# Value heads 1 to 3 of the gated linear branch as one job of seven half-size products

## The chip, the cores and the metric

The kernel runs on one core of a Trainium2 chip. The metric is the device time of one execution in microseconds (us). A core has a matrix engine (TensorE, PE in the profile; PEld are its weight loads), a vector engine (DVE), a scalar engine (ACT), GpSimd (POOL) and SyncE (SP), which here issues the DMA transfers. Each engine works through its own list of instructions in order and waits on semaphores for the others. Matrix products accumulate in PSUM banks; everything else is held in SBUF.

## The reference

One layer of a decoder with two parallel token mixers, for 1024 tokens and a width of 1024, in float32:

```
h = rmsnorm(x, norm_g)
proj = h @ w_in                        # one wide projection, split into
g_q, g_k, g_v, g_gate, g_rank, s_q, s_k, s_v, s_gate, m_logits
log_a = log_sigmoid(g_rank @ w_dec_up + b_dec) / 16
o_gla = gla_chunked(g_q, g_k, g_v, log_a)          # 4 heads, values of 256
o_gla = rmsnorm(o_gla, gla_norm_g) * silu(g_gate);  y_a = o_gla @ w_pa
o_sb = stick_breaking(s_q, s_k, s_v) * silu(s_gate); y_b = o_sb @ w_pb
merged = g_a * y_a + g_b * y_b                      # sigmoid gates
x = rmsnorm(x + merged @ w_o, final_g)
```

The case is about g_v, the values of the first branch: h (1024 x 1024) times 1024 columns of w_in, four heads of 256 columns. The decay code g_rank has 16 columns and rides along with head 0.

## The kernel before

**Precision.** Every float32 factor is split into a high half (ACT, L163: a copy to the matmul's type, names ending in h) and a low half (DVE, L164: the value minus its high half, names ending in l). A product is three matmuls: high x high, high x low, low x high.

**First stage (0 to 44.6 us).** For each of eight blocks of 128 tokens (tb): ACT sums the squares, DVE scales the sum, POOL takes the power -1/2 (L229, a tile r of 128 x 1), DVE multiplies by r and the gain (L397, xs), PE transposes (L417), and ACT and DVE split the result into the quarters of h. There are four quarters, by half of the tokens and by parity of the 128-wide feature blocks: A11, A12, A21, A22, named ha11, ha12, ha21, ha22 in the trace, each with four blocks j. One block behind, PE computes head 0 with the decay code for the previous block (272 columns). ACT's and DVE's order is that of the code; the other engines' order is set by the scheduler at build time.

**The value heads 1 to 3 (44.6 to 113.8 us).** 24 units, one for each head and token block, are plain projections (L221): 24 matmuls of 256 columns each, tokens on the output's partitions, eight feature blocks deep. DVE splits each result straight out of PSUM and SP stores it. Meanwhile POOL makes sums of the quarters of h that later jobs need: A11, A12, A21, A22 as whole values (L502, high plus low) and S1, S2, S3, S4 from them (L505), 32 operations of 512 elements a row; ACT and DVE split the S.

**The pairs (from 113.8 us).** All other projections are jobs of two heads that use seven products of half size instead of eight (Winograd's form of Strassen's scheme): weights as the stationary side, sums T1 to T4 of weight quarters made on POOL (L241 to L244, tt), seven units per job, 512 columns a matmul. Between the units of the first jobs stand the decay steps: `wup`, the decay's up-projection, is loaded (L655), put into a stack (`wst`, L668 and L670), the decay codes are transposed (L677) and split into `rst`, and L684 multiplies both (logits). Job 0's loads and its first three splits stand at the head, ahead of the decay steps.

Of the kernel before, what the change touches and what calls it, by code (L numbers as in the profile page):

```python
# [101 lines left out]
def hybrid_layer(ctx: ExitStack, tc: tile.TileContext, x, norm_g, w_in, w_up, b_dec,  # L102
# [355 lines left out]
    vw = v_ctx.enter_context(tc.tile_pool(name="vw", bufs=2, reuse_waits="tile"))  # L458
    vws, vraw = {}, {}

    def v_load(c0, key):
        vraw[key] = raw_tile()
        nc.sync.dma_start(vraw[key], w_in[:, c0:c0 + DV].rearrange("(k p) c -> p k c", p=P))

    def v_split(key, i):

        hi, lo = ((vw.tile([P, 4, DV], F32R, tag="v" + s, name="v" + s) if i else
                   w_tile(s).rearrange("p k c -> p (k c)").rearrange("p (k c) -> p k c", c=DV)) for s in "hl")
        split(vraw[key][:, 4 * i:4 * i + 4], hi, lo)
        vws.setdefault(key, []).append((hi, lo))  # L470
# [10 lines left out]
    vjobs = [(i, C_GV + i * DV) for i in range(1, GLA_H)]  # L481
    v_load(vjobs[0][1], vjobs[0][0])
    v_load(vjobs[1][1], vjobs[1][0])
    vline = []
    for i, (key, _) in enumerate(vjobs):
        for tb in range(NT):
            vline.append((lambda key=key, tb=tb: v_unit(key, tb), True))
            if tb in (3, 4) and i + 1 < len(vjobs):
                vline.append((lambda key=vjobs[i + 1][0], a=tb - 3: v_split(key, a), False))
# [1005 lines left out]
```

## Time and profile before

| | |
|---|---|
| time, median of 3 runs | 1190.39 us (1189.76 to 1190.4) |
| profiled execution, span | 1187.3 us |
| PE busy | 1174.5 us (99%) |
| DVE busy | 834.8 us (70%) |
| POOL busy | 294.4 us (25%) |
| value heads 1 to 3 | 576 matmuls, 69.33 us |

The profiled execution is shown by its span; no other time of it is recorded, and the runs are about 3 us longer than the span. A row of a timeline has the start, the time of the instruction or group, engine, line, operation, tiles (written, then read), shape, and count; in square brackets the idle time of the engine before it and what ended that. L numbers are lines of the kernel before. In the changed kernel the same helpers have other numbers (split is L160 and L161, the power L226).

### The profile page before, as it was taken

The page shows a single profiled execution, that of the slowest core. Times are in us where ns is not written, and L with a number is a line of the kernel's source. Part 1 is how long each engine was busy: PE and PEld are TensorE (multiplying, and loading weights), DVE is VectorE, ACT ScalarE, POOL GpSimd, SP SyncE. Part 2 cuts the span into 40 slices and gives each one's busy share as a digit, 9 for nine tenths or more (in the row PEclk, how much of TensorE's full clock was granted, in tenths as well). Part 3 has the DMA queues.
Part 4 walks back from the last instruction along what each step waited for, and adds up shares of the span by engine and source line. Part 5 has one row for each costly group of instructions (what it writes and reads, how often), then busy time and mean ns, then how long its engine had stood idle before and what let it go on. Part 6 is the DMA issues. An engine that isn't in the chain of part 4 may idle for free.

```text
span 1187.3 us, 17020 instructions
## 1 busy us (share of the span) xinstructions
PE 1174.5 (99%) x6051; PEld 989.3 (83%) x6051; DVE 834.8 (70%) x1388; ACT 535.3 (45%) x1000; POOL 294.4 (25%) x249
## 2 busy tenths in 40 slices
PE   8999999999999999999999999999999999999997
PEld 8999878888888888888888887888888888888886
DVE  6475876787677777767656567547787876488986
ACT  5343763333444444444434444334444544275543
POOL 1496513143333233224223223000000000700001
PEclk9999999999999999999999999999999999999999
DMA  7434349998356566655454447899766556848652
GB/s 286 196 133 153 129 164 317 331 316 275 120 187 222 183 213 215 188 187 169 145 168 149 133 138 229 254 322 320 258 218 224 186 168 192 288 160 285 220 195 106
DMA packets 189377, 247.65 MB, mean 209 GB/s; under 512 B 12358, under 2 KB 121948, under 8 KB 187756
## 3 DMA queue, kind: packets, MB, share of 16 engines
q1 hardware_dynamic: 188716, 245.52, 61.6%
q8 instruction: 47, 0.77, 0.3%
q10 hardware_dynamic: 576, 1.05, 0.2%
q14 instruction: 38, 0.31, 0.1%
HBM read 154.25 MB, written 92.27 MB: 208 GB/s over the span
## 4 chain that ended last, share of the span: by engine, by line
PE 89%; DVE 4%; ACT 2%; DMA 2%; issue 1%; SPq 0%; POOL 0%; ACTq 0%; DVEq 0%
PE pp L268 15%; PE pp L269 15%; PE pp L270 15%; PE pp L221 8%; PE pp L204 3%; PE pp L203 3%; PE pp L202 3%; PE tr L990 1%; PE av L1013 1%; PE av L1012 1%; PE av L1011 1%; PE z L972 1%; PE z L974 1%; PE z L973 1%; PE xb L1379 1%
## 5 line engine op out<-in xcount | busy, mean ns | idle before, releaser
L164 DVE TENSOR_TENSOR wl<-tt,wh 128x1024 fp32r<-128x1024 f32 x62 | 77.5, 1250 | 53.2 <-ACT wh L163 52.9
L307 DVE TENSOR_TENSOR f<-pp,f 128x512 f32<-128x512 f32 x93 | 64.0, 688 | 72.1 <-PE pp L270 68.2
L242 POOL TENSOR_TENSOR tt<-raw 128x512 f32<-128x512 f32 x31 | 44.6, 1438 | 225.2 <-DVE wl L164 204.8
L163 ACT ACTIVATE wh<-tt 128x1024 fp32r<-128x1024 f32 x62 | 65.6, 1058 | 74.7 <-PE pp L269 68.8
L274 ACT ACTIVATE f<-pp 128x512 f32<-128x512 f32 x93 | 55.1, 593 | 88.2 <-PE pp L270 84.9
L978 DVE TENSOR_TENSOR_SCAN be<-be,m 128x128 f32<-128x128 f32 (+3 forms) x64 | 86.1, 1347 | 4.5 <-ACT be L975 4.3
L163 ACT ACTIVATE wh<-raw 128x1024 fp32r<-128x1024 f32 x44 | 46.5, 1059 | 84.0 <-PE pp L269 48.1
L164 DVE TENSOR_TENSOR wl<-raw,wh 128x1024 fp32r<-128x1024 f32 x44 | 64.3, 1463 | 18.7 <-ACT wh L163 18.1
L229 POOL TENSOR_TENSOR r<-r,nhalf 128x1 f32<-128x1 f32 x40 | 24.4, 609 | 198.3 <-DVE r L228 177.2
L1162 POOL TENSOR_TENSOR N<-A,A 128x512 f32<-128x512 f32 x4 | 6.6, 1658 | 244.0 <-PE pp L204 244.0
L975 ACT ACTIVATE be<-z 128x384 f32<-128x384 f32 (+4 forms) x96 | 47.1, 495 | 19.7 <-PE z L974 17.3
L268 PE MATMUL pp<-ha11h,wh 128*128 128x512 f32 x124 | 49.2, 397 | 0.0
L268 PE MATMUL pp<-S2h,wh 128*128 128x512 f32 x124 | 49.1, 396 | 0.0
L268 PE MATMUL pp<-S1h,wh 128*128 128x512 f32 x124 | 49.1, 396 | 0.0
L268 PE MATMUL pp<-ha12h,wh 128*128 128x512 f32 x124 | 49.0, 395 | 0.0
L268 PE MATMUL pp<-ha22h,wh 128*128 128x512 f32 x124 | 48.9, 394 | 0.2 <-DVE f L307 0.2
L268 PE MATMUL pp<-S3h,wh 128*128 128x512 f32 x124 | 48.8, 394 | 0.0
L268 PE MATMUL pp<-S4h,dh 128*128 128x512 f32 x124 | 48.6, 392 | 0.0
L270 PE MATMUL pp<-S1h,wl 128*128 128x512 f32 x124 | 48.4, 390 | 0.0
L270 PE MATMUL pp<-ha11h,wl 128*128 128x512 f32 x124 | 48.4, 390 | 0.0
L269 PE MATMUL pp<-S2l,wh 128*128 128x512 f32 x124 | 48.3, 390 | 0.0
L270 PE MATMUL pp<-ha12h,wl 128*128 128x512 f32 x124 | 48.3, 390 | 0.0
(519 smaller groups left out, 3844.4 us busy)
## 6 DMA issues: line engine op xcount, KB each, us to landing
raw<-in_w_in_dram SPq DMA_DIRECT2D x34, 1024.0 KB, 6.0
d_gv<-o SPq DMA_DIRECT2D x16, 512.0 KB, 2.6
d_t<-t SPq DMA_DIRECT2D x16, 512.0 KB, 6.4
v<-d_gv SPq DMA_DIRECT2D x32, 256.0 KB, 3.0
d_ogl<-o SPq DMA_DIRECT2D x64, 128.0 KB, 2.6
d_q<-o SPq DMA_DIRECT2D x16, 512.0 KB, 3.8
d_k<-o SPq DMA_DIRECT2D x16, 512.0 KB, 3.5
d_v<-o SPq DMA_DIRECT2D x32, 256.0 KB, 2.5
```

The lines of the kernel that those rows point to most:

```text
L163: nc.scalar.activation(hi, src, AF.Copy)
L164: eng.tensor_sub(lo, src, hi.bitcast(F32))
L202: nc.tensor.matmul(pt, whi[:, kb], h_, start=kb == 0, stop=False)
L221: nc.tensor.matmul(pt[:, 0:n], *ops[kb][i], start=k == 0, stop=k == 3 * KB - 1)
L242: nc.gpsimd.tensor_sub(t1, b[:, 0, 1], b[:, 0, 0])
L268: nc.tensor.matmul(pt, bh[:, j], ah[:, j], start=first and j == 0, stop=False, skip_group_check=True)
L269: nc.tensor.matmul(pt, bh[:, j], al[:, j], start=False, stop=False, skip_group_check=True)
L270: nc.tensor.matmul(pt, bl[:, j], ah[:, j], start=False, stop=j == 3, skip_group_check=True)
L274: nc.scalar.activation(t[nm], t[bank], AF.Copy)
L307: nc.vector.tensor_add(add, bank, add)
L975: nc.scalar.activation(om[:, off + pc * w:off + (pc + 1) * w], zt[:, 0:w], AF.Sigmoid, scale=-inv_sqrt)
L978: nc.vector.tensor_tensor_scan(rest, rest, m1[:, off:T][:, ::-1], 1.0, op0=ALU.mult, op1=ALU.max)
```

## The change

Heads 1 to 3 become one job of 768 columns, computed with the same seven-product scheme, but with tokens on the output's partitions: the features are the stationary side and the weights move. Weight quarters are B11, B12, B21, B22 (parity of the feature block by half of the columns, 384 each). A product u has two halves (jp, two feature blocks each) of four token blocks t: 56 items k of six matmuls of 384 columns, 336 in all.

DVE makes the weight sums T1, T2, T4, T3 (1536 elements a row), splits the weights in pieces of 768 and the S in pieces of 512. POOL makes the sums of the features in another order: of A11 and A12 as whole values before the job (`whole`), the others inside it. Results are evicted by product: product 0 and products 2, 3 are copied by ACT, product 1 is added to product 0's copy and stored, product 5 is added out of two banks and stored, and the last product (u = 6) is added to both kept ones and stored, eight times. A store (`v_put`) is a high half, a low half and two transfers, since 384 columns reach over a head and a half.

Job 0 of the pairs gets its loads and first splits at items 40 to 55 instead of at its start. In the job the orders of ACT, DVE and PE are those of the code (a table `due` of items); POOL's and SP's are set by the scheduler. The x tiles, the weights of head 0 and the quarters of the sums are laid out anew in SBUF.

```diff
-        for j in self.jobs[:2]:
-            j["load"]()
-        for s in range(3):
-            self.jobs[0]["split"][s]()
+        self.first = [j["load"] for j in self.jobs[:2]] + self.jobs[0]["split"][:3]
...
+    VH = 3 * DV // 2
+    VPRODUCTS = [("A11", "B11"), ("A12", "B21"), ("A22", "T4"), ("S1", "T1"), ("S2", "T2"), ("S4", "B22"), ("S3", "T3")]
+    vq, vsp = {}, {}
...
+    def vq_split(u, jp):
+        src = vq[VPRODUCTS[u][1]][:, 2 * jp:2 * jp + 2]
+        hi, lo = (w_tile(s).rearrange("p k c -> p (k c)")[:, 0:2 * VH].rearrange("p (j c) -> p j c", c=VH) for s in "hl")
+        split(src, hi, lo)
+        vsp[u, jp] = hi, lo
+
+    def vq_sum(nm):
+
+        x1, x2_, where = {"T1": ("B12", "B11", "B11"), "T2": ("B22", "T1", None), "T4": ("B21", "T2", "B21"),
+                          "T3": ("B22", "B12", "B12")}[nm]
+        dst = vq[where] if where else vq_tile(nm)
+        nc.vector.tensor_sub(dst, vq[x1], vq[x2_])
+        vq[nm] = dst
+
+    def whole(dst, q, j):
+        nc.gpsimd.tensor_add(dst, q[0][:, j].bitcast(F32), q[1][:, j].bitcast(F32))
+
+    VW_AT = {4: (0, 0), 5: (0, 1), 6: (1, 0)}
...
+                if tb >= 4:
+                    if tb == 4:
+                        w11 = slot(4, [P, 4 * HALF], "w11").rearrange("p (j t) -> p j t", j=4)
+                    whole(w11[:, tb - 4], hq[0, 0], tb - 4)
+                if tb in VW_AT:
+                    vq_split(*VW_AT[tb])
...
-    def v_unit(i, tb):
-        st = v_stage(i, tb)
-        split(proj_n(rows_of(vws[i]), hq, tb), st[:, 0], st[:, 1])
-        store_v(i, i, tb)
...
-        ops = [whole("a21", hq[1, 0], j), whole("a22", hq[1, 1], j), sum2("S1", "a21", "a22", ALU.add),
-               whole("a11", hq[0, 0], j), sum2("S3", "a11", "a21"), sum2("S2", "S1", "a11"),
-               whole("a12", hq[0, 1], j), sum2("S4", "a12", "S2")]
-        at = [(8 * j + i) * 22 // 32 for i in range(8)]
-        for i, op in enumerate(ops):
-            line[at[i]].append(op)
-        for i, nm in ((2, "S1"), (4, "S3"), (5, "S2"), (7, "S4")):
-            line[at[i] + 2].insert(0, part(nm, j))
...
+    def h_sum(nm, j):
+        if nm == "S1":
+            a22, x21[j] = (ev.tile([P, HALF], F32, tag="f", name="f") for _ in range(2))
+            whole(a22, hq[1, 1], j)
+            whole(x21[j], hq[1, 0], j)
+            nc.gpsimd.tensor_add(w1[:, j], x21[j], a22)
+        elif nm == "S3":
+            nc.gpsimd.tensor_sub(x21[j], w11[:, j], x21[j])
+        elif nm == "S2":
+            nc.gpsimd.tensor_sub(w11[:, j], w1[:, j], w11[:, j])
+        else:
+            whole(w12[:, j], hq[0, 1], j)
+            nc.gpsimd.tensor_sub(w12[:, j], w12[:, j], w11[:, j])
...
+    def v_put(n, J, t, c):
+
+        o = stage()[:, :, 0:VH]
+        split(c, o[:, 0], o[:, 1])
+        tb = 4 * n + t
+        for h, c0, o0, w in (((1, 0, 0, DV), (2, 0, DV, P)) if J == 0 else ((2, P, 0, P), (3, 0, P, DV))):
+            nc.sync.dma_start(d_gv[h][:, tb, :, c0:c0 + w], o[:, :, o0:o0 + w].bitcast(F32))
...
+    def v_item(u, jp, t, bank):
+        (ah, al), (bh, bl) = comb[VPRODUCTS[u][0]], vsp[u, jp]
+        ts = slice(t * P, (t + 1) * P)
+        for i in range(2):
+            j = 2 * jp + i
+            nc.tensor.matmul(bank, ah[:, j, ts], bh[:, i], start=u < 4 and j == 0, stop=False, skip_group_check=True)
+            nc.tensor.matmul(bank, ah[:, j, ts], bl[:, i], start=False, stop=False, skip_group_check=True)
+            nc.tensor.matmul(bank, al[:, j, ts], bh[:, i], start=False, stop=j == 3, skip_group_check=True)
...
+    def v_evict(u, t):
+        if u == 0:
+            nc.scalar.activation(s1[:, t, 0:VH], vx[t], AF.Copy)
+        elif u == 1:
+            nc.vector.tensor_add(s1[:, t, 0:VH], vy[t], s1[:, t, 0:VH])
+            v_put(0, 0, t, s1[:, t, 0:VH])
+        elif u in (2, 3):
+            nm = ("p7", "s5")[u - 2]
+            if t == 0:
+                keep4[nm] = vq_tile(nm)
+            nc.scalar.activation(keep4[nm][:, t], vy[t], AF.Copy)
+        elif u == 5:
+            c = sw.tile([P, 4, P], F32, tag="d" + "hl"[t % 2], name="c", bufs=1).rearrange("p a c -> p (a c)")[:, 0:VH]
+            nc.scalar.activation(c, vy[t], AF.Copy)
+            nc.vector.tensor_add(c, vx[t], c)
+            v_put(0, 1, t, c)
+        elif u == 6:
+            for J, nm in ((1, "s5"), (0, "p7")):
+                c = keep4[nm][:, t]
+                nc.vector.tensor_add(c, vx[t], c)
+                v_put(1, J, t, c)
...
+    for k, nm in ((0, "T1"), (2, "T2"), (6, "T4"), (14, "T3")):
+        at(k, vq_sum, nm)
+    at(5, vq_split, 1, 1)
+    for u in range(2, 7):
+        at(8 * u - 7, vq_split, u, 0)
+        at(8 * u - 4 if u == 4 else 8 * u - 3, vq_split, u, 1)
+    for nm, ks in (("S1", (16, 18, 20, 22)), ("S2", (26, 28, 31, 33)), ("S4", (34, 36, 39, 41)), ("S3", (42, 44, 46, 47))):
+        for j in range(4):
+            at(ks[j], h_split, nm, j)
+    for u in range(7):
+        if u != 4:
+            for t in range(4):
+                due[8 * u + 5 + t].insert(0, (v_evict, (u, t)))
+    for k, fn in zip((40, 46, 49, 53, 55), pairs.first):
+        at(k, fn)
+    manual = ExitStack()
+    manual.enter_context(tc.manual_schedule(engines={mybir.EngineType.Activation, mybir.EngineType.DVE,
+                                                     mybir.EngineType.PE}))
+    for j in range(4):
+        h_sum("S1", j)
+    for j in range(4):
+        h_sum("S3", j)
+        h_sum("S2", j)
+    for j in range(4):
+        h_sum("S4", j)
+    for k in range(60):
+        if k < 56:
+            u, r = divmod(k, 8)
+            jp, t = divmod(r, 4)
+            if jp == 0:
+                bank = v_bank(u, t)
+            else:
+                bank = vx[t] if u in (0, 4, 6) else vy[t]
+            v_item(u, jp, t, bank)
+        for fn, args in due[k]:
+            fn(*args)
```

Three places in the engines' lists. First POOL in the first stage; r is the root of a token block, ha11 and ha12 are quarters of h, w_494 is the whole A11 and w_701 the whole A12, f are temporaries. Before:

```order
L229 TENSOR_TENSOR r<-r,nhalf 128x1 x8
L502 TENSOR_TENSOR f<-ha21h,ha21l 128x512
L502 TENSOR_TENSOR f<-ha22h,ha22l 128x512
L505 TENSOR_TENSOR f<-f 128x512
L502 TENSOR_TENSOR f<-ha11h,ha11l 128x512
```

With the change:

```order
L226 TENSOR_TENSOR r<-r,nhalf 128x1 x5
L390 TENSOR_TENSOR w_494<-ha11h,ha11l 128x512 x4
L390 TENSOR_TENSOR w_701<-ha12h,ha12l 128x512 x2
L226 TENSOR_TENSOR r<-r,nhalf 128x1
L390 TENSOR_TENSOR w_701<-ha12h,ha12l 128x512 x2
L226 TENSOR_TENSOR r<-r,nhalf 128x1 x2
L390 TENSOR_TENSOR f<-ha22h,ha22l 128x512
```

Six sums now stand between the fifth and the sixth root, and two more ahead of the last two.

Second, DVE around products 0 and 1 of the new job (there is no such place before). wl are low halves of weights; T_764 is T2, the sum into raw from T_764 is T4, the sum into raw from B_696 (B22) is T3; s_702 is the sum of products 0 and 1, o the stored low half:

```order
L386 TENSOR_TENSOR T_764<-B_696,vq 128x1536
L161 TENSOR_TENSOR wl<-raw,wh 128x768
L386 TENSOR_TENSOR raw<-raw,T_764 128x1536
L161 TENSOR_TENSOR wl<-raw,wh 128x768
L676 TENSOR_TENSOR s_702<-pp,s_702 128x384
L161 TENSOR_TENSOR o<-s_702,o 128x384
L161 TENSOR_TENSOR wl<-raw,wh 128x768
L676 TENSOR_TENSOR s_702<-pp,s_702 128x384
L161 TENSOR_TENSOR o<-s_702,o 128x384
L386 TENSOR_TENSOR raw<-B_696,raw 128x1536
L676 TENSOR_TENSOR s_702<-pp,s_702 128x384
L161 TENSOR_TENSOR o<-s_702,o 128x384
```

The adds that free product 1's banks (L676) stand between the weight sums and the weight splits; the third stands behind T3.

Third, DVE at the end of the value heads; wst is the stack of the decay's up-projection, rst that of the codes. Before:

```order
L164 TENSOR_TENSOR S3l<-f,S3h 128x512
L164 TENSOR_TENSOR o<-pp,o 128x256 x2
L164 TENSOR_TENSOR S4l<-f,S4h 128x512
L670 TENSOR_TENSOR wst<-wup,wst 16x512
L670 TENSOR_TENSOR rst<-tr,rst 16x512
L164 TENSOR_TENSOR wl<-tt,wh 128x1024
```

With the change (s_1019 and p_942 are the two kept quarters; two more such groups of four stand ahead of these rows):

```order
L691 TENSOR_TENSOR s_1019<-vx,s_1019 128x384
L161 TENSOR_TENSOR o<-s_1019,o 128x384
L691 TENSOR_TENSOR p_942<-vx,p_942 128x384
L161 TENSOR_TENSOR o<-p_942,o 128x384
L161 TENSOR_TENSOR dl<-raw,dh 128x512
L691 TENSOR_TENSOR s_1019<-vx,s_1019 128x384
L161 TENSOR_TENSOR o<-s_1019,o 128x384
L691 TENSOR_TENSOR p_942<-vx,p_942 128x384
L161 TENSOR_TENSOR o<-p_942,o 128x384
L760 TENSOR_TENSOR wst<-wup,wst 16x512
L760 TENSOR_TENSOR rst<-tr,rst 16x512
```

The first decay stack now stands behind eight adds and eight low halves of the last product. In SP's list the load of wup stands behind the job's last store, and in PE's list the first logit matmul stands behind 36 matmuls of job 0 and the eight transposes of the codes.

More of the change, by code (lines that the diff above doesn't have):

```diff
@@ L403, in hybrid_layer @@
             load_x(tb)
+        for nm in ("B11", "B21", "B12"):
+            vq_load(nm)
         def first_v(tb):
@@ L457, in hybrid_layer @@
     v_ctx = ExitStack()
[L458 to L470, printed above, removed]
-    def v_unit(i, tb):
-        st = v_stage(i, tb)
-        split(proj_n(rows_of(vws[i]), hq, tb), st[:, 0], st[:, 1])
-        store_v(i, i, tb)
+    vw = v_ctx.enter_context(tc.tile_pool(name="vw", bufs=1, reuse_waits="tile"))
     def ch3(a):
@@ L480, in hybrid_layer @@
     ebl = const.tile([P, GLA_H, NCH], F32, tag="ebl", name="ebl")
[L481 to L489, printed above, removed]
-            if tb == 5 and i + 2 < len(vjobs):
-                vline.append((lambda job=vjobs[i + 2]: v_load(job[1], job[0]), False))
-    st = Line(vline)
-    f = {}
-    def fresh(nm):
-        f[nm] = ev.tile([P, HALF], F32, tag="f", name="f")
-        return f[nm]
-    def whole(nm, q, j):
-        return lambda: nc.gpsimd.tensor_add(fresh(nm), q[0][:, j].bitcast(F32), q[1][:, j].bitcast(F32))
-    def sum2(nm, a, b, op=ALU.subtract):
-        return lambda: nc.gpsimd.tensor_tensor(fresh(nm), f[a], f[b], op=op)
-    def part(nm, j):
-        def go():
-            if nm not in comb:
-                comb[nm] = quarter(a21b, nm, "a21") if nm == "S2" else quarter(sp, nm, nm.lower())
-            split(f[nm], comb[nm][0][:, j], comb[nm][1][:, j])
-        return go
-    line = [[] for _ in range(25)]
-    for j in range(4):
-        ops = [whole("a21", hq[1, 0], j), whole("a22", hq[1, 1], j), sum2("S1", "a21", "a22", ALU.add),
-               whole("a11", hq[0, 0], j), sum2("S3", "a11", "a21"), sum2("S2", "S1", "a11"),
-               whole("a12", hq[0, 1], j), sum2("S4", "a12", "S2")]
-        at = [(8 * j + i) * 22 // 32 for i in range(8)]
-        for i, op in enumerate(ops):
-            line[at[i]].append(op)
-        for i, nm in ((2, "S1"), (4, "S3"), (5, "S2"), (7, "S4")):
-            line[at[i] + 2].insert(0, part(nm, j))
-    manual = ExitStack()
-    manual.enter_context(tc.manual_schedule(engines={mybir.EngineType.Activation, mybir.EngineType.DVE}))
-    for a in range(2):
-        v_split(vjobs[0][0], a)
-    st.run(1)
+    vq_load("B22")
     for i, s in enumerate("hl"):
         nc.sync.dma_start(d_a21[i], hq[1, 0][i].bitcast(F32))
-    for ops in line:
-        for op in ops:
-            op()
-        st.run(1)
-    manual.close()
     def qk_pair(c0, i, dst):
@@ L637, in gla_qk @@
         return [gqk_pair(C_GQ, i, inv_sqrt, d_e1, d_gq), gqk_pair(C_GK, i, 1.0, d_e2, d_gk)]
-    st.run()
-    v_ctx.close()
-    a21_ctx.close()
     late = []
@@ new lines, in hybrid_layer, with at @@
+    due = {k: [] for k in range(60)}
+    def at(k, fn, *args):
+        due[k].append((fn, args))
+    for k, nm in ((0, "T1"), (2, "T2"), (6, "T4"), (14, "T3")):
[7 more added lines that the diff above has]
+            at(ks[j], h_split, nm, j)
```

38 lines of the change are left out of this document (36 added, 2 removed).

## The prediction

> **What bounds the kernel now.** I read the page first (busy shares, then the shares of the chain that ended last), next a table of four stretches around the change, then that chain near the job, and last single rows.
>
> ```profile
> span 1187.3 us, 17020 instructions
> PE 1174.5 (99%) x6051; PEld 989.3 (83%) x6051; DVE 834.8 (70%) x1388; ACT 535.3 (45%) x1000; POOL 294.4 (25%) x249
> PE 89%; DVE 4%; ACT 2%; DMA 2%; issue 1%; SPq 0%; POOL 0%; ACTq 0%; DVEq 0%
> ```
>
> TensorE (PE) is busy 1174.5 of 1187.3 us: whatever makes it pause adds to the end, whatever takes matmuls from it shortens it. In the stretches below the columns are the busy time of PE, PE's weight loads, DVE, ACT and POOL, then clock, DMA share and GB/s.
>
> ```profile
> 24.50:44.50 20.00, 19.98 (x157) 19.03 (x155) 13.47 (x28) 9.38 (x19) 5.14 (x6) 1.00 0.32 134
> 44.60:113.80 69.20, 69.20 (x578) 69.19 (x578) 39.86 (x49) 24.19 (x47) 51.25 (x34) 1.00 0.45 161
> 82.20:94.45 12.25, 12.25 (x104) 12.25 (x103) 12.25 (x11) 5.72 (x11) 11.85 (x6) 1.00 0.67 223
> 113.80:135.00 21.20, 21.20 (x99) 17.13 (x97) 14.50 (x18) 14.97 (x20) 8.40 (x8) 1.00 0.16 63
> ...
> 44.64 69.33 PE pp L221 x576
> 113.98 1.73 DMA wup<-in_w_dec_up_dram
> ```
>
> In the second half of the first stage, in the job and behind it PE never stops. Inside the job (44.60 to 113.80) DVE has 29 us to spare, but in its third row DVE and POOL are both full. The last two rows are the chain: 576 matmuls of 256 columns in 69.33 us, 0.1204 each; and then a DMA that the change will move.
>
> **What is saved.** The new job issues 336 matmuls of 384 columns. The trace has no such width; it has 512 columns:
>
> ```profile
> 126.64 0.39 PE L268 MATMUL pp<-S3h,wh 128*128 128x512 f32 x1
> ...
> 129.36 0.39 PE L268 MATMUL pp<-S4h,dh 128*128 128x512 f32 x1
> ```
>
> Twelve matmuls lie between these two starts: 2.72/12 = 0.2267 each. Halfway between 0.1204 and 0.2267 is 0.1735, so the job costs 336 x 0.1735 = 58.3 us instead of 69.3: **-11.0 us** if PE is always fed. The rest is whether it is. I call the start of the job S and its end E; S to E was 69.3, and 58.3 is the floor.
>
> **Part A, the first stage.** POOL makes the inverse root r of each token block (L229). As built, POOL's order is now five r, four sums of A11, two of A12, and only then the sixth r (token block 5).
>
> ```profile
> 23.04 0.55 POOL L229 TENSOR_TENSOR r<-r,nhalf 128x1 f32<-128x1 f32 x1 [3.42 <-DVE r L228]
> 27.52 0.55 POOL L229 TENSOR_TENSOR r<-r,nhalf 128x1 f32<-128x1 f32 x1 [3.93 <-DVE r L228]
> ...
> 40.93 1.29 POOL L502 TENSOR_TENSOR f<-ha21h,ha21l 128x512 f32<-128x512 f32 x1 [4.96 <-DVE ha21l L164]
> 42.17 1.31 POOL L502 TENSOR_TENSOR f<-ha22h,ha22l 128x512 f32<-128x512 f32 x1
> ...
> 23.28 1.23 DVE L164 TENSOR_TENSOR wl<-raw,wh 128x1024 fp32r<-128x1024 f32 x1 [0.39 <-ACT wh L163]
> 24.43 0.68 DVE L164 TENSOR_TENSOR ha11l<-tr,ha11h 128x512 fp32r<-128x512 f32 x1
> 25.03 0.68 DVE L164 TENSOR_TENSOR ha12l<-tr,ha12h 128x512 fp32r<-128x512 f32 x1
> ...
> 29.60 1.28 DVE L397 SCALAR_TENSOR_TENSOR xs<-xt,r,gb 128x1024 f32<-128x1024 f32 x1
> ...
> 31.02 1.06 PE L417 MATMUL tr<-ident,xs 128*128 128x128 f32 x8
> 34.94 1.06 PE L417 MATMUL tr<-ident,xs 128*128 128x128 f32 x8
> ```
>
> The sixth r ran at 27.52. The first sum needs the last low half of the first four blocks, ha11l, done at 25.1; I take 24.5, since the weight split at 23.28 is no longer ahead of it. Six sums at 1.24 (40.93 to 42.17) take 7.4, xs of block 4 holds one up by 1.2, and r takes 0.55: r of block 5 is done at 33.7 instead of 28.1. DVE's xs of that block, ahead of everything later in its order, then ends at 34.9, or 36.2 if the next sum is ahead of it, instead of 30.88; the transposes, at 31.02 before and in order on PE, follow it. That is +4.0 to +5.3, and about 0.7 for a next block that starts late too. Lowest +3 (the sums start earlier than I take it), highest +6.5. **I take +4.7.**
>
> **Part B, inside the job.** DVE reads two SBUF operands in sums of 1536 elements (T2, T4, T3), low halves of 768 (weights), 512 (S) and 384 (outputs); POOL has 24 sums of 512.
>
> ```profile
> 109.17 0.69 DVE L164 TENSOR_TENSOR S2l<-f,S2h 128x512 fp32r<-128x512 f32 x1
> ...
> 62.79 1.30 POOL L505 TENSOR_TENSOR f<-f 128x512 f32<-128x512 f32 x1 [1.83 <-DVE S3l L164]
> ...
> 63.09 1.54 DVE L164 TENSOR_TENSOR S2l<-f,S2h 128x512 fp32r<-128x512 f32 x1
> ...
> 87.61 1.78 DVE L164 TENSOR_TENSOR S4l<-f,S4h 128x512 fp32r<-128x512 f32 x1
> 91.02 2.32 DVE L164 TENSOR_TENSOR wl<-tt,wh 128x1024 fp32r<-128x1024 f32 x1
> ...
> 108.65 0.42 DVE L164 TENSOR_TENSOR o<-pp,o 128x256 fp32r<-128x256 f32 x1 [2.45 <-ACT o L163]
> ```
>
> Alone a 512 low half takes 0.69. While POOL sums it takes 1.54 or 1.78, and a 1024 one 2.32 instead of 1.23: 63.09 begins 0.3 behind POOL's sum of 62.79 and ends 0.54 after it. In the window from 82.20 an average of about 0.87 us is added per such operation (1.1, 1.1, and less for others), so that is the price I use; the ends are nothing and a whole POOL sum, 1.27. From 0.69 for 512 and 1.23 for 1024 (0.60 and 1.14 from one start to the next, as 24.43 to 25.03 has it) I get 0.87 for 768, 1.68 for 1536 and 0.47 for 384.
>
> T2 needs B22, whose load now stands behind the first stage's last store and takes 6 us (the page's median of the 1 MB weight loads, quoted below): T2 starts near S+7.3. DVE's fixed order then gives, each with 0.87 on top: T2 to 9.9, a weight split to 11.6, T4 14.1, a weight split 15.9, the first add of product 1 at 16.4, its output split 18.2, a weight split 19.9, the second add 20.4, its split 22.2, T3 24.8, third add 25.2, split 27.0, fourth add 27.5. Product 2 needs these adds to have its PSUM banks back, and its fourth block would start at S+19.8 (item 19): it waits until 27.5, **7.7 us**. Product 3 waits for the low halves of S1 behind that: two of them and a weight split end near S+34, against 32.7 for PE, 1.3 more. From there the splits keep ahead, with 25.0 us for the last three products and about 1 for late banks: E = S+68.5, that is **-0.8 against 69.3**. With nothing added per operation the same walk has the fourth add near S+21: E = S+60, -9.3. With a full 1.27 it is S+73: +4.
>
> The Trainium skill, page "SBUF — State Buffer", section "Who interferes with whom", says that an exclusive lock covers the whole instruction when DVE has two SBUF inputs and GpSimd reads SBUF. By it the sum below would take the +4 end, 4.8 more. The row at 63.09 agrees with it; the mean of 0.87 in the window from 82.20 is milder.
>
> **Part C, behind the job.** The last product (both kept quarters, four blocks) is evicted by eight steps: DVE add, ACT high half, DVE low half, store. In DVE's order they stand one behind the other, and each low half waits for ACT.
>
> ```profile
> 506.00 0.69 DVE L307 TENSOR_TENSOR f<-pp,f 128x512 f32<-128x512 f32 x1 [0.57 <-PE pp L270]
> ...
> 506.77 0.63 ACT L163 ACTIVATE o<-f 128x512 fp32r<-128x512 f32 x1 [0.37 <-DVE f L307]
> ...
> 507.44 0.69 DVE L164 TENSOR_TENSOR o<-f,o 128x512 fp32r<-128x512 f32 x1
> ...
> raw<-in_w_in_dram SPq DMA_DIRECT2D x34, 1024.0 KB, 6.0
> ...
> 118.37 0.68 DVE L670 TENSOR_TENSOR rst<-tr,rst 16x512 fp32r<-16x512 f32 x1 [1.23 <-ACT rst L668]
> ...
> 120.18 0.39 PE L684 MATMUL tr<-rst,wst 128*128 128x512 f32 x1
> ```
>
> At 512 the low half starts 1.44 after its add; at 384 I scale to 1.15, plus 0.47 for itself: 1.62 a step, 13.0 for eight, and 2.6 for two splits of the next pair job that stand between them. The first block's bank is full three blocks of 1.04 before E, at E-3.1, so the last low half ends at E+12.5. The decay codes stand behind that on three queues: SP issues wup's load behind the last of 32 stores (+0.7), DVE makes its low half and that of rst behind the puts. Before, issue at 113.98 to rst's low half at 119.05 took 5.07. So the first logit matmul can start at E+18.3. PE's order has 36 matmuls of 512 columns (8.2) and eight transposes (0.9, from 1.06 per eight) ahead of it: there at E+9.0, and everything behind it waits in order. **+9.3**; before, there was no such pause (21.20 of 21.20 busy). Lowest +4 (shorter steps, 1.2 each, and the load earlier), highest +12.
>
> **Sum.** -11.0 is already inside B. A +4.7, B -0.8, C +9.3: +13.2. The profiled execution has span 1187.3, and the runs are 1190.39, 3.1 above it; I add to the runs: 1190.4 + 13.2 = **1203.6**.
>
> **Rivals.**
> *DVE keeps pace inside the job* (0.18): nothing is added beside POOL, B is -9.3, A and C stay: +4.7, 1195. For it: bank reads such as 108.65 stay at 0.42. Against it: 63.09 and 87.61.
> *The vector engine is never late* (0.10), the other side: the same free port, and eviction steps shorter than I scale: the mechanism is that DVE follows PE within its own durations. Place: the puts of products 1 and 6; price: B -10, A +2, C +4, so -4, 1186.4; it decides as soon as the three pauses sum to less than 11.0. At best 1179.4. For it: DVE's spare 29 us. Against it: POOL's order in A and the serial puts stand in the program whatever the durations are.
> *Pauses cost more than their length* (0.12): A and C leave PE idle 4 and 9 us. At the start of the run:
>
> ```profile
> 1.42 5.91 PE L147 MATMUL warm<-ident 128*128 128x128 f32 x26 [1.42 <-POOL ident masks.py:199]
> 8.47 1.06 PE L147 MATMUL warm<-ident 128*128 128x128 f32 x8
> ```
>
> The same matmul takes 0.227 at first and 0.133 later: 26 x 0.094 = 2.4 us after an idle PE. Twice that, +4.9: 1208.5. Against it: the granted clock reads 1.00 in every stretch quoted. The page "TensorE: Matmul & The Clock Gate" of the Trainium skill, "Part 1: The HAM clock gate", has such a slow restart after an idle window; the two rows agree with it.
>
> **How the numbers follow.** Forecast 0.60, its own range 1197 to 1211; rivals 0.18, 0.10, 0.12. A measurement of this kernel tells 0.2%, 2.4 us, from no change. Faster: the second rival, 0.10. Within 0.2%: the low part of the first, 0.03. Slower: the rest, 0.87. The range of 8 in 10 is 1193 to 1214: it takes in the first rival and the clock's price, and leaves out the faster side and the sum of all highest ends (+22.5).
>
> **What would show it.** A: a PE gap of some 5 us ahead of the transposes of block 5, ended by xs, with POOL sums ahead of r. B: product 2 waiting for adds behind T3; low halves of 512 over 1 us where POOL sums; job length near 68. C: a PE gap near 9 us ahead of the first logit matmul, released by rst. It is wrong if the job runs near 59 us, if POOL's r runs near 28, or if the codes' splits come ahead of the puts.

## The result and the profile after

The changed kernel takes 1222.44 us (median of 4 runs, 1220.49 to 1223.72), the kernel before 1190.32 in the same comparison: a ratio of 1.0264, 95% interval 1.024 to 1.0289. It is 32.1 us slower. The prediction was 1203.6 with a range of 1193 to 1214: its sign and its three places were right, and it was too small by 18.8.

The page of the changed kernel, the rows that answer to those shown of before:

```profile
span 1220.7 us, 16624 instructions
PE 1175.0 (96%) x5811; PEld 985.4 (81%) x5811; DVE 864.3 (71%) x1408; ACT 545.9 (45%) x1016; POOL 300.8 (25%) x249
PE 80%; DVE 8%; DMA 4%; ACT 4%; issue 3%; POOL 1%; SPq 0%; ACTq 0%; DVEq 0%; POOLq 0%
```

Two numbers of it tell most. PE was idle for 12.8 us before (1187.3 - 1174.5) and is for 45.7 now (1220.7 - 1175.0). And PE is as long busy as before, 1175.0 against 1174.5, although the job has 11.0 us fewer matmuls: some 11.5 us have come on elsewhere, most of it matmuls that run slowly.

The timeline of PE in the changed kernel has the places. In square brackets is the idle time and what ended it:

```profile
27.10 1.07 PE L455 MATMUL tr<-ident,xs 128*128 128x128 f32 x8 [0.62 <-DVE xs L433]
...
35.99 1.94 PE L455 MATMUL tr<-ident,xs 128*128 128x128 f32 x8 [4.93 <-DVE xs L433]
...
51.50 0.44 PE L668 MATMUL vx<-wh,ha11h 128*128 128x384 f32 x1
...
71.08 0.44 PE L668 MATMUL pp<-wh,ha22h 128*128 128x384 f32 x1 [1.62 <-DVE s L676]
...
75.43 0.69 PE L668 MATMUL pp<-wh,ha22h 128*128 128x384 f32 x1 [3.03 <-DVE s L676]
75.92 0.52 PE L669 MATMUL pp<-wl,ha22h 128*128 128x384 f32 x1
76.24 0.52 PE L670 MATMUL pp<-wh,ha22l 128*128 128x384 f32 x1
...
98.54 0.69 PE L670 MATMUL vx<-wh,S2l 128*128 128x384 f32 x1 [2.79 <-DVE S2l L161]
...
126.61 0.39 PE L265 MATMUL pp<-ha11h,wh 128*128 128x512 f32 x1
...
138.43 0.61 PE L767 MATMUL tr<-ident,rcode 128*16 128x128 f32 x4 [3.00 <-DVE p L691]
148.80 0.79 PE L774 MATMUL tr<-rst,wst 128*128 128x512 f32 x1 [9.77 <-DVE rst L760]
149.59 0.79 PE L265 MATMUL pp<-S2h,wh 128*128 128x512 f32 x1
150.18 0.63 PE L266 MATMUL pp<-S2l,wh 128*128 128x512 f32 x1
150.61 0.63 PE L267 MATMUL pp<-S2h,wl 128*128 128x512 f32 x1
```

The job starts at 51.50 instead of 44.57 (+6.9) and ends, with the first matmul of pair job 0, at 126.61 instead of 114.15: 75.1 us against 69.6 (+5.5). The stretch behind it costs another 17.2; I measure it to the first matmul of the last pair job, at 776.29 before and at 805.91 now. That makes 29.6. The other 3.8 of the span stand in the last third of the program, which the change does not touch.

The slow matmuls are seen behind the longer pauses. Behind 75.43 one of 384 columns starts every 0.32 us; in an undisturbed place of the same job it is 0.173. Behind 148.80 one of 512 columns starts every 0.43, against 0.227. The granted clock (the share of full speed that the profile has for PE) of the stretch from 70 to 80 says the same, the last three numbers being clock, DMA share and GB/s:

```profile
70.00:80.00 10.00, 5.40 (x18) 4.57 (x19) 8.13 (x8) 2.80 (x6) 10.00 (x6) 0.71 0.65 206
```

### The profile page after: what moved, and what is told of

The parts are those of the page before. It is cut to its first block, busy times and chain, and to the rows that moved or that the text cites. A ratio compares the mean times of both kernels' runs of the same rounds, so it can differ in the third digit from the quotient of the medians.

```text
span 1220.7 us, 16624 instructions
## 1 busy us (share of the span) xinstructions
PE 1175.0 (96%) x5811; PEld 985.4 (81%) x5811; DVE 864.3 (71%) x1408; ACT 545.9 (45%) x1016; POOL 300.8 (25%) x249
## 4 chain that ended last, share of the span: by engine, by line
PE 80%; DVE 8%; DMA 4%; ACT 4%; issue 3%; POOL 1%; SPq 0%; ACTq 0%; DVEq 0%; POOLq 0%
PE pp L265 15%; PE pp L266 15%; PE pp L267 15%; PE pp L199 3%; PE pp L200 3%; PE pp L201 3%; PE av L1103 1%; PE av L1102 1%; DVE wl L161 1%; PE av L1101 1%; PE z L1062 1%; PE tr L1080 1%; PE xb L1467 1%; PE xb L1469 1%; PE z L1063 1%
## 5 line engine op out<-in xcount | busy, mean ns | idle before, releaser
L239 POOL TENSOR_TENSOR tt<-raw 128x512 f32<-128x512 f32 x31 | 44.6, 1438 | 228.7 <-DVE wl L161 221.8
L160 ACT ACTIVATE wh<-raw 128x1024 fp32r<-128x1024 f32 (+1 forms) x47 | 48.5, 1032 | 90.9 <-PE pp L266 50.4
L161 DVE TENSOR_TENSOR wl<-raw,wh 128x1024 fp32r<-128x1024 f32 (+1 forms) x47 | 66.6, 1418 | 21.8 <-ACT wh L160 21.0
L242 POOL TENSOR_TENSOR tt<-raw,tt 128x512 f32<-128x512 f32 x31 | 48.8, 1574 | 2.3
L267 PE MATMUL pp<-S2h,wl 128*128 128x512 f32 x124 | 48.7, 393 | 0.0
```

The costliest lines, as they stand in the source:

```text
L160: nc.scalar.activation(hi, src, AF.Copy)
L161: eng.tensor_sub(lo, src, hi.bitcast(F32))
L239: nc.gpsimd.tensor_sub(t1, b[:, 0, 1], b[:, 0, 0])
L242: nc.gpsimd.tensor_sub(t4, b[:, 1, 0], t2)
L267: nc.tensor.matmul(pt, bl[:, j], ah[:, j], start=False, stop=j == 3, skip_group_check=True)
```

## The experiments

All times are compared with 1222.44 (the changed kernel) and, where said, with one another. The table takes each profile apart at the same three points as above: start of the job, its length, what the stretch behind costs over before's 662.14 (from pair job 0 to the last pair job), and the rest to the end of the span. Two columns more are of use inside the job: the time from its start to the matmul of product 4 that needs S2's second low half (S2), where PE waits 1.3 to 2.8 us in all kernels but e4 and e10, and PE's mean granted clock in the job. Neither the change nor any edit touches the rest, and yet it runs from 411.1 to 416.6, so an edit is best read from the places, and the median counts only where it moves by more. e4, e9 and e10 leave out work.

| kernel | median us | against before (95%) | job starts | job | S2 | clock | behind | rest |
|---|---|---|---|---|---|---|---|---|
| before | 1190.32 | | 44.57 | 69.6 | | 1.00 | 0 | 411.0 |
| changed | 1222.44 | 1.0264 (1.024 to 1.0289) | 51.50 | 75.1 | 47.0 | 0.91 | 17.2 | 414.8 |
| e1 POOL in written order | 1214.28 | 1.0201 (1.0186 to 1.0217) | 44.97 | 75.9 | 46.5 | 0.91 | 17.6 | 413.5 |
| e2 T3 late | 1216.54 | 1.0219 (1.0204 to 1.0234) | 52.48 | 71.1 | 44.3 | 1.00 | 17.3 | 412.0 |
| e3 codes before the puts | 1213.13 | 1.0193 (1.0178 to 1.0209) | 51.96 | 75.8 | 47.0 | 0.93 | 9.3 | 412.3 |
| e4 no POOL sums | 1200.88 | 1.0086 (1.0069 to 1.0103) | 43.99 | 64.8 | 36.7 | 0.97 | 17.2 | 412.6 |
| e5 the three mends | 1205.07 | 1.0117 (1.0098 to 1.0137) | 48.06 | 73.4 | 42.7 | 0.93 | 8.5 | 411.5 |
| e6 and adds first | 1205.32 | 1.0129 (1.0104 to 1.0153) | 47.91 | 70.3 | 42.7 | 0.95 | 10.6 | 416.6 |
| e7 and sum in PSUM | 1200.86 | 1.0088 (1.0073 to 1.0103) | 46.48 | 68.3 | 41.6 | 0.98 | 10.7 | 412.3 |
| e8 filled pause | 1233.93 | 1.0379 (1.0344 to 1.0414) | 51.17 | 76.6 | 47.1 | 0.89 | 29.8 | 413.9 |
| e9 e7 without last evictions | 1191.02 | 1.0004 (0.9993 to 1.0014) | 46.51 | 68.1 | 41.4 | 0.97 | 0.1 | 412.1 |
| e10 e7 without POOL sums | 1192.80 | 1.0025 (1.0015 to 1.0035) | 43.97 | 62.0 | 36.1 | 1.00 | 10.6 | 412.3 |
| e11 e7, one sum per root | 1203.31 | 1.0115 (1.0097 to 1.0133) | 44.97 | 69.4 | 41.3 | 0.98 | 10.6 | 413.4 |
| e12 the change again | 1216.94 (1 run) | | 51.07 | 73.8 | 47.1 | 0.93 | 17.1 | 411.1 |

**e1: POOL follows the written order.**

```diff
-        with tc.manual_schedule(engines={mybir.EngineType.Activation, mybir.EngineType.DVE}):
+        with tc.manual_schedule(engines={mybir.EngineType.Activation, mybir.EngineType.DVE, mybir.EngineType.Pool}):
```

(the same addition in the job)

> POOL follows the written order in the first stage and in the job: the roots r come ahead of the sums of A11, the four sums of A12 move into the job. In the changed kernel the job starts at 51.50 instead of 44.57. Theory 1 (the pause of the first stage is POOL's order and nothing else): the job starts at 44.6 to 46, no PE gap ahead of the transposes of block 5, and the total falls by 5 to 7 us. Rival (the port between DVE and POOL must carry the sums anyway, so the time is given back in the job): the start moves as above, but the job grows from 75.1 by 4 to 6 us, total -2 to +1.

The job starts at 44.97, the gaps of 0.62 and 4.93 are gone, and the job is 0.8 longer with four more sums in it. That is 5.3 less at the three places, within theory 1's 5 to 7; the median is 8.2 less. Theory 1 holds, and little of the time is given back. The timeline of POOL in the changed kernel has the cause:

```profile
22.99 0.55 POOL L226 TENSOR_TENSOR r<-r,nhalf 128x1 f32<-128x1 f32 x1 [3.44 <-DVE r L225]
24.58 6.01 POOL L390 TENSOR_TENSOR w<-ha11h,ha11l 128x512 f32<-128x512 f32 x4 [1.04 <-DMA vrow<-in_b_gate_dram]
30.55 2.48 POOL L390 TENSOR_TENSOR w<-ha12h,ha12l 128x512 f32<-128x512 f32 x2
32.99 0.54 POOL L226 TENSOR_TENSOR r<-r,nhalf 128x1 f32<-128x1 f32 x1
```

A root of half a microsecond stands behind 8.4 us of sums that nobody needs until the job runs.

**e2: the weight sum T3 later.**

```diff
-    for k, nm in ((0, "T1"), (2, "T2"), (6, "T4"), (14, "T3")):
+    for k, nm in ((0, "T1"), (2, "T2"), (6, "T4"), (34, "T3")):
```

> The weight sum T3 moves from item 14 to item 34, nothing else. Theory 1 (DVE's chain beside POOL's sums is what the job waits for, up to the second low half of S2 at 98.5): T3's 2.8 us leave that chain, S2's low half comes near 95.7, job 75.1 becomes 71 to 73, total -2.5 to -4. Theory 2 (the wait of 3.03 us of product 2 for the add behind T3, with the slow matmuls that follow it, is the cost): job -5 to -7. Rival (POOL's sums set the S, DVE only follows): no change within 1 us.

The job falls from 75.1 to 71.1, by 4.0, and the total by 5.9, of which 2.8 stand in the rest. The gap of 3.03 went, but PE waits as long in all (9.9 in both jobs): new waits of 0.4 to 0.7 came up in product 3, which is ready earlier than its S1, and S2's low half is still waited for, 44.3 behind the job's start instead of 47.0. These 2.7 are the edit's, as theory 1 had it: the chain of DVE operations, not the one add, is what the job waits for. The other 1.3 are of the slow clock, which followed that wait in the changed kernel and not here. The clock is 1.00 in the whole job (third number from the end):

```profile
52.48:123.57 71.09, 61.20 (x338) 57.91 (x337) 53.79 (x53) 30.04 (x56) 45.88 (x28) 1.00 0.32 103
```

**e3: the decay codes ahead of the last evictions.**

```diff
+    at(38, code_load)
+    at(39, code_room)
+    at(50, code, 0)
+    at(51, code, 1)
...
-    djobs = [[(code, 0)], [(code, 1)]]
+    djobs = [[], []]
```

> The load of wup, its stack and the stacks of the decay codes are made at items 38 to 51, ahead of the eight evictions of the last product, in the room that B22 leaves; the code transposes use another PSUM bank. Theory 1 (the pause behind the job is the codes standing behind the puts): the gap of 9.8 us ahead of the first logit matmul and the 3.0 ahead of the code transposes go, total -12 to -17. Rival (the eight evictions hold PE up anyway, through the banks and pair job 0's splits behind them): the gap only moves, total -3 to -6.

The stretch behind costs 9.3 instead of 17.2, the total is 9.3 less, 2.5 of it in the rest. Theory 1 wanted 12 to 17, the rival 3 to 6: both are in it. The wait of 9.8 for rst is gone. What PE waits for in its place, in microseconds, times and the longest, from 127 to 182:

```profile
PE pp L265 <- DVE f L304: 3.3, 1, 3.3
PE pp L265 <- ACT f L271: 2.1, 2, 1.5
PE tr L785 <- DVE p L693: 1.5, 1, 1.5
```

These are pair job 0's and 1's own evictions and the last product's adds: DVE and ACT are behind.

**e4: no sums on POOL.**

```diff
     def whole(dst, q, j):
-        nc.gpsimd.tensor_add(dst, q[0][:, j].bitcast(F32), q[1][:, j].bitcast(F32))
+        pass
...
+        src = hq[{"S1": (1, 1), "S2": (0, 0), "S3": (1, 0), "S4": (0, 1)}[nm]][0][:, j].bitcast(F32)
```

(and `h_sum`, which makes S1 to S4 on POOL, does nothing)

> Leaves out all 32 sums of the features on POOL: S1 to S4 are split from the high halves of A22, A11, A21, A12 instead, so DVE and ACT do the same number of operations of the same shapes. Theory 1 (POOL's sums and DVE's two-input operations exclude each other): low halves of 768 take 0.96 instead of 2.0, of 512 0.69 instead of 1.78; the job starts near 44.6 and takes 59 to 62 us instead of 75.1, total -19 to -23. Rival (DVE's order and ACT alone are too long, POOL hardly matters): the job starts near 44.6 but still takes 70 to 74, total -7 to -11.

The job starts at 43.99 and takes 64.8 instead of 75.1; the total is 21.6 less. So POOL costs 10.3 us of the job and all of the first pause, and 6.5 of the job above 58.3 have other causes (T3's place among them). It is not that the sums come late: in the changed kernel's job no wait of ACT or DVE is put down to POOL. The job was somewhat longer than theory 1 had it, and far below the rival. DVE's timeline of this kernel holds both cases, since pair job 0's own sums still run on POOL from 71.16 to 77.8:

```profile
70.12 0.96 DVE L161 TENSOR_TENSOR wl<-vq,wh 128x768 fp32r<-128x768 f32 x1
71.02 0.69 DVE L161 TENSOR_TENSOR S1l<-ha22h,S1h 128x512 fp32r<-128x512 f32 x1
72.91 2.02 DVE L161 TENSOR_TENSOR wl<-T,wh 128x768 fp32r<-128x768 f32 x1 [1.20 <-ACT wh L160]
74.86 1.77 DVE L161 TENSOR_TENSOR S2l<-ha11h,S2h 128x512 fp32r<-128x512 f32 x1
76.69 1.90 DVE L161 TENSOR_TENSOR wl<-T,wh 128x768 fp32r<-128x768 f32 x1
78.52 0.68 DVE L161 TENSOR_TENSOR S2l<-ha11h,S2h 128x512 fp32r<-128x512 f32 x1
```

The same shapes take 0.96 and 0.69 with POOL silent, 2.02 and 1.77 beside it: 1.06 and 1.08 more for each. The Trainium skill, page "SBUF — State Buffer", section "Who interferes with whom", has this as an exclusive lock between a DVE instruction with two SBUF inputs and a GpSimd instruction that reads SBUF; the rows agree.

**e5: the three mends together.** e1's order with two sums behind each root instead of one, e2's T3, e3's codes.

> The three edits together on the changed kernel: POOL in the written order, with the eight whole sums two behind each root of blocks 5 to 7 and the last two behind; T3 at item 34; the decay codes ahead of the last evictions. Theory 1 (three separate costs): 6.5 + 4.0 + 7.9 us less as measured one by one, 18.4 in all, so near 1204. Rival (they share DVE's time, so that what one frees another takes): 12 to 14 less, near 1209.

1205.07, 17.4 less than the changed kernel. That looks like theory 1, but 3.3 of it stand in the rest; at the three places it is 13.8 less, the rival's number. The job starts at 48.06, 3.1 later than in e1, with two gaps of 0.8 ahead of transposes that wait for xs beside the second sum. It takes 73.4, 2.3 more than in e2, although S2's low half comes 1.6 earlier: two stretches of slow clock stand behind that wait here, none in e2.

**e6: both adds ahead of both low halves.**

```diff
-            for J, nm in ((1, "s5"), (0, "p7")):
+            for nm in ("s5", "p7"):
                 c = keep4[nm][:, t]
                 nc.vector.tensor_add(c, vx[t], c)
-                v_put(1, J, t, c)
+            for J, nm in ((1, "s5"), (0, "p7")):
+                v_put(1, J, t, keep4[nm][:, t])
```

(and product 5's split one item after its add)

> As the three mends, and the evictions of the last product make both adds of a block ahead of both low halves, and product 5's output split comes one item after its add. The same operations in another order. Theory 1 (behind the job DVE idles while it waits for ACT's high half in each of eight serial steps, 0.6 each, and what stands behind it is late by that): 4 to 7 us less than the three mends alone. Rival (PE waits behind the job for banks and for pair job 0's own evictions, whatever the order of the puts): less than 1.5 less.

No gain: 1205.32 against 1205.07. The job is 3.0 shorter, all of it behind the wait for S2's low half: product 5's banks are waited for 0.30 instead of 1.84, and there is one slow stretch fewer. The stretch behind the job, where theory 1 expected the gain, is 2.1 longer. Theory 1 falls.

**e7: product 1's sum in PSUM.**

```diff
-            nc.vector.tensor_add(s1[:, t, 0:VH], vy[t], s1[:, t, 0:VH])
-            v_put(0, 0, t, s1[:, t, 0:VH])
+            nc.vector.tensor_add(vy[t], vy[t], s1[:, t, 0:VH])
+            v_put(0, 0, t, vy[t])
```

> As the run with both adds first, and product 1's sum is written back into its PSUM bank and split from there, so that the four output low halves (1.7 us each beside POOL) have one SBUF operand only. Theory 1 (the port): these low halves take 0.55, the low half of S2 that product 4 waits for comes 3 to 4.5 us earlier, total 2 to 4.5 less. Rival (product 2 waits for the banks, which are now held until the low half is made): no gain, up to 1.5 more.

4.5 less than e6: the job is 2.0 shorter and starts 1.4 earlier, the latter nothing that the edit does. The four low halves take 0.56, as theory 1 had it, but S2's low half comes only 1.1 earlier (41.6 behind the job's start instead of 42.7) and not 3 to 4.5; the other 0.9 of the job is mainly a slow stretch behind that wait, which e6 has and e7 has not. So some 1 us is shown to be the edit's, less than theory 1 gave. Product 2 waits for the banks now (1.76 and 1.24 for the low half), as the rival said; PE waits 5.6 in all in both jobs.

**e8: matmuls in the pause.**

```diff
+            for _ in range(56 if (h, n) == (0, 0) else 0):
+                nc.tensor.matmul(pt[:, 0:P], ident, ident, start=True, stop=True)
```

> The changed kernel with 56 extra matmuls of 128 columns on the identity put into the pause of 9.8 us ahead of the first logit matmul; they write columns of a bank that the logit overwrites. Theory 1 (after a pause PE runs slow for some us: the 512-column matmuls start every 0.43 instead of 0.227 for about nine of them): with the pause filled they start every 0.23 at once, the stretch behind is 1.5 to 2.2 us shorter, total -1 to -2. Rival (these matmuls are slow because they wait for operands): no change in their spacing, total 0 to +1.

The filling failed: the extra matmuls waited for the same bank and came behind the pause (9.71, as before), so the total is 11.5 more. It tells the two apart all the same, since the 512-column matmuls now follow other matmuls and not the pause. The timeline of PE (two records for each of the 56 matmuls):

```profile
149.91 15.46 PE L775 MATMUL tr<-ident 128*128 128x128 f32 x112 [9.71 <-DVE rst L760]
165.13 0.71 PE L776 MATMUL tr<-rst,wst 128*128 128x512 f32 x2
165.68 0.39 PE L265 MATMUL pp<-S2h,wh 128*128 128x512 f32 x1
165.91 0.40 PE L266 MATMUL pp<-S2l,wh 128*128 128x512 f32 x1
```

They start every 0.23 at once. From the first logit matmul to the next job's first matmul it is 3.7 us (165.13 to 168.87) against 5.8 in the changed kernel (148.80 to 154.63): a restart after this pause costs 2.1 us. In e8 the operands too had more time, but the changed kernel's granted clock says that they are not the reason. It is 0.50 just there:

```profile
148.80:152.70 3.90, 3.90 (x8) 2.57 (x9) 3.25 (x5) 2.85 (x5) 2.31 (x2) 0.50 0.00 0
```

The Trainium skill, page "TensorE: Matmul & The Clock Gate", section "Part 1: The HAM clock gate", has half the rate after an idle window until PE has been busy for about 3.4 us. Here 0.43 against 0.227 is a factor of 1.9, and it lasts from 148.80 to 152.7, 3.9 us: the rows agree.

**e9: e7 without the last product's evictions.** The adds and splits of product 6 are left out; the stores go out of the kept quarters.

> As the run with the sum in PSUM, but it leaves out the adds, high halves and low halves of the last product's eight evictions; the same stores go out of the kept quarters instead. There the stretch behind the job costs 10.7 us against the kernel before, although the decay codes come early. Theory 1 (these eight evictions fall into a stretch in which DVE and ACT have no room for them; the decay steps and pair job 0's evictions behind them are late, and PE waits): without them that cost is 0 to 2.5, total 8 to 10 less than with them. Rival (pair job 0's splits and the decay steps are late for another reason, the end of the job coming earlier than their data): 1 to 4 less.

9.8 less than e7, and the stretch behind costs 0.1: theory 1 in full. The first 21 us behind the job, e7 first and then e9; the third and the fourth entry are DVE and ACT:

```profile
114.80:136.00 21.20, 18.24 (x77) 13.80 (x77) 19.37 (x27) 11.86 (x20) 6.91 (x6) 1.00 0.56 172
```

```profile
114.63:135.50 20.87, 20.36 (x90) 16.41 (x90) 16.18 (x18) 14.50 (x19) 6.06 (x4) 1.00 0.30 102
```

DVE had 6.7 us to spare in the same stretch before (14.50 of 21.20). With the eight evictions it is busy for 19.37, and the pair jobs' own evictions come late: of PE's waits in e7 between 114.8 and 170, 6.9 us are for these (3.8 for ACT's copies, 3.1 for DVE's adds) and 1.1 for banks of the last product; in e9 0.5 is left.

**e10: e7 without sums on POOL**, left out as in e4.

> As the run with the sum in PSUM, and all 32 sums on POOL left out as before (S split from high halves). Theory 1 (shared port): with DVE's order mended and POOL silent the job runs at the matmuls' own pace, 58.3 to 60.5 instead of 68.3, and starts at 44.6; total 9 to 12 less than with the sums. Rival (a wait of DVE and PE on each other that has nothing to do with POOL, such as the banks of products 1 and 2): the job stays at 63 to 66, total 4 to 7 less.

8.1 less than e7, between theory 1 (9 to 12) and the rival (4 to 7); the job takes 62.0, between them too (58.3 to 60.5 and 63 to 66). So most of what e7's job has above 58.3 is POOL's, and what is left are waits for banks, as the rival had it, in products 2 and 6. PE stops seven times for a moment, four of them shown as waits of 0.3 us, two of these

```profile
62.26 0.45 PE L661 MATMUL pp<-wh,ha22h 128*128 128x384 f32 x1 [0.34 <-DVE o L161]
63.89 0.45 PE L661 MATMUL pp<-wh,ha22h 128*128 128x384 f32 x1 [0.32 <-DVE o L161]
```

With the job's first matmul and the slower ones behind each stop, all that is above 0.173 comes to 3.7, and 58.3 is left, the arithmetic's number.

**e11: one sum behind each root, decay steps two units later.**

> As the run with the sum in PSUM, with one sum behind each root in the first stage (the sums of A12 move into the job) and the decay steps two units later. Theory 1 (both places have DVE time to win): the job starts 1.5 earlier, the stretch behind costs 2 to 4 less, total 3 to 5 less, near 1196.5; still slower than the kernel before. Rival (the four sums in the job and the shifted steps cost as much as they free): within 1.5 of 1200.9.

No gain: 1203.31 against e7's 1200.86, 2.4 more and so even above the rival's 1.5. The job does start 1.5 earlier, and is 1.1 longer; the four sums do not delay S2's low half (41.3 instead of 41.6), but a slow stretch follows that wait here. The stretch behind costs 10.6 as before, so the shifted steps gain nothing there, as the rival had it; that they only move DVE's load is an argument and was not tested.

**e12: the changed kernel once more.**

> The changed kernel itself, profiled a second time. In its first profile 29.6 of the 33.4 us stand ahead of the last third of the program and 3.8 in it, where the change touches nothing; in the experiments that last third was 0.5 to 5.6 longer than before. Theory 1 (the last third differs from one execution to the next): the first part is again 29 to 30.5 later, the last third differs from the first profile's 414.8 by more than 1 us. Rival (the change lengthens it, by another placement): 414.5 to 415.1 again.

The last third takes 411.1, what it took before the change, and not 414.8: the 3.8 us there differ from one execution to the next. The job was 73.8 here, 1.3 less than in the first profile, and 27.9 us instead of 29.6 stand ahead of the last pair job, a little below the 29 to 30.5 expected. The 1.3 are the clock behind the same wait for S2's low half (2.79 and 2.83 us), first in the changed kernel and then here:

```profile
98.54:101.50 2.96, 2.96 (x9) 2.96 (x10) 2.37 (x4) 2.80 (x6) 0.00 (x0) 0.50 0.00 0
```

```profile
98.14:101.50 3.36, 3.36 (x19) 3.36 (x20) 2.77 (x4) 2.81 (x6) 0.00 (x0) 1.00 0.00 0
```

So the three parts are known to some 1.3 us each. This one execution is 5.5 below the median of the first four, so a difference of that size from 1222.44 is not by itself an edit's.

No version that does the whole work beats the kernel before; the best, e7, is 0.9% slower.

## Why the prediction was wrong

**Direction, places and the saving were right.** The 384-column matmul starts every 0.173 us, as interpolated, so 11.0 us were saved; the three costs stand where parts A, B and C put them. The sizes were +6.9, +5.5 and +17.2 instead of +4.7, -0.8 and +9.3. What failed: in all three parts the slow restart behind a pause was put at nothing; in B the splits of S2 were said to keep ahead; in C the load of wup was priced at 1.73, and the last evictions were not counted as a load on DVE.

**A, 4.7 against 6.9: the pause was right, the restart was missing.** The sixth root was predicted for 33.7 and came at 33.5; the gap of 4.93 lies inside "+4.0 to +5.3". The block that starts behind it takes 5.8 us (35.99 to 41.80) instead of 3.92, because the transposes and the first matmuls run slowly (granted clock 0.50 from 36 to 40). The term "about 0.7 for a next block" stood for another thing, a next block that starts late; that did not come, and the slow restart of 1.9 stands in its place.

**B, -0.8 against +5.5: the walk was right as far as it went, and ended too early.** T2 starts 6.5 us behind the job's start (predicted 7.3), the fourth add ends at 26.7 (27.5), product 3 starts at 34.9 (34), product 4 at 43.2 (42.3). Up to here it is 0.9 late. The price of 0.87 holds as a mean: over the 20 operations with two SBUF operands from T2 to the low half of S2 that product 4 waits for, the changed kernel takes 0.87 more for each than the same shapes in e4 (1.76, 0.56, 0.69 and 0.96). It is not one price, though. DVE's timeline, and then POOL's:

```profile
65.99 0.99 DVE L161 TENSOR_TENSOR wl<-raw,wh 128x768 fp32r<-128x768 f32 x1 [0.97 <-ACT wh L160]
...
68.04 0.56 DVE L161 TENSOR_TENSOR o<-s,o 128x384 fp32r<-128x384 f32 x1 [0.59 <-ACT o L160]
...
72.09 2.82 DVE L386 TENSOR_TENSOR raw<-B,raw 128x1536 f32<-128x1536 f32 x1
...
76.02 1.68 DVE L161 TENSOR_TENSOR o<-s,o 128x384 fp32r<-128x384 f32 x1 [0.64 <-ACT o L160]
...
80.40 1.77 DVE L161 TENSOR_TENSOR S1l<-w,S1h 128x512 fp32r<-128x512 f32 x1
...
82.09 2.03 DVE L161 TENSOR_TENSOR wl<-vq,wh 128x768 fp32r<-128x768 f32 x1
...
96.74 1.75 DVE L161 TENSOR_TENSOR S2l<-w,S2h 128x512 fp32r<-128x512 f32 x1
```

```profile
66.12 2.00 POOL L631 TENSOR_TENSOR f<-w,f 128x512 f32<-128x512 f32 x1
68.09 1.64 POOL L390 TENSOR_TENSOR f<-ha21h,ha21l 128x512 f32<-128x512 f32 x1
```

An operation that starts while one of POOL's has just begun loses 1.06 to 1.12; those at 65.99 and 68.04 start as one of POOL's ends and lose nothing, and the next of POOL's takes 2.00 and 1.64 instead of 1.28. From the fourth add on each loses some 1.08. The step that failed is "From there the splits keep ahead". Carried on at its own 0.87, the walk has an output split, four splits of S1, four of weights and two of S2 behind the fourth add at 27.5, and so the last of these near 44.6. The matmul that needs it is the sixth of product 4, at 43.2 in the prediction: already a wait. The low half came at 47.0, 3.8 behind that; POOL was still at work, since pair job 0's four sums follow on it until 97.9. Behind it come 1.5 of slow clock, and 1.9 instead of "about 1" of waits for product 5's banks. The slow matmuls between 75.43 and 84.46 (4.0) stand ahead of the wait for S2's low half, and DVE does not wait for PE there, so they cost the job nothing.

The rule of the Trainium skill (page "SBUF — State Buffer", section "Who interferes with whom"), an exclusive lock for the whole instruction, was taken in the prediction as the +4 end. The rows agree with the rule, and the mean is 0.87 all the same; the walk's +4 at the full price is short of +5.5 too, since neither the restart nor the waits behind its end are in it.

**C, 9.3 against 17.2: the queue was right, its consequences were cut short.** The last low half was predicted for 12.5 us behind the end of the job and came 13.0 behind (139.57). Then the load of wup took 4.72 instead of 1.73, and the chain of waits shows it on the path:

```profile
140.01 0.63 SPq L650
...
140.69 4.72 DMA wup<-in_w_dec_up_dram
...
145.57 0.58 issue
146.15 0.63 ACT wst L758
```

So the logit came 22.2 us behind the end of the job, not 18.3, and 3.0 of these 3.9 are the load. (The code transposes waited for banks of the last product too, 3.00, but were done at 139.0, ahead of the load, and add nothing.) After that the sum stopped, and the trace does not: 2.1 us of restart and 1.3 of small waits behind it. The DMA engines were 0.77 busy while it ran (140.69 to 145.4), 0.11 at the same load before, with the job's last stores just ahead of it; that these held it up is likely and was not tested. The larger omission is that the pause was put down to the codes alone. e3 and e9 show that these are half of it: with the codes early, 8.5 to 10.7 us remain, and without the evictions of the last product 0.1. I had counted these evictions only as something that the codes stand behind, not as a load on DVE in a stretch that has 6.7 us to spare.

**The rivals.** The third, "pauses cost more than their length", was given 0.12 and argued against with a granted clock of 1.00. That number came from stretches without a pause, which say nothing on one. e8 and the clock rows show the mechanism. Its price was near: 1.9 in A, 1.5 in B and 2.1 in C make 5.5, against the 4.9 given, and it belonged into every part that predicts a pause, as a term of the sum. Even so 1208.5 is 13.9 too low, so this alone was not what failed. The two rivals in which DVE keeps pace fall with the rows above; e4 shows that work on POOL beside DVE's is the larger cause inside the job.

## What to carry to other kernels

Where PE is 99% busy, saved matmuls are worth their time only if every engine around them keeps pace: list for each new wait its length, and add the slow restart behind it where nothing later is waited for anyway. When work is moved off one stretch, look at which engine has to do the rest of it and in which stretch: here DVE had 29 us to spare inside the job and 6.7 behind it, and the change put the last evictions where there was little. And a short operation that many wait for (the root, the decay codes) must stand ahead of long ones in its engine's queue, whoever sets that queue's order.

## What the runs showed of the hardware

A pause of PE was dearer than I had expected: behind one of 4.9 us the next block lost 1.9, behind one of 9.8 the next matmuls 2.1, and behind 1.6 and 3.0 close to each other 25 matmuls lost 4.0 (0.32 instead of 0.173 each). There the half clock lasted 9.0 us (75.43 to 84.46) with a single break of 0.5 in it, longer than the 3.9 behind 148.80. So the about 3.4 us of the Trainium skill, quoted at e8, do not hold behind every pause here. Nor does the length of a pause alone decide: a wait of 2.8 us for the same low half of S2 was followed by slow matmuls in the changed kernel (98.54, 0.69 for the first) and by quick ones in e12 and in e2:

```profile
96.81 0.44 PE L670 MATMUL vx<-wh,S2l 128*128 128x384 f32 x1 [2.83 <-DVE S2l L161]
```

And a DVE operation with two SBUF operands beside POOL loses, whatever its own length, what is left of POOL's current operation when it starts, less 0.14 us. In the changed kernel T2 (58.02) starts 0.64 ahead of that end and loses 0.50, T3 (72.09) 1.21 and 1.06, the split at 82.09 1.22 and 1.07, the one at 65.99 0.17 and 0.03. So with POOL never idle a short operation loses as much as a long one, and many short ones suffer most.
